# Subtracting the row maximum in a streaming softmax: one DVE maximum per tile, 12 tile buffers, unsplit last stores

## The chip, the cores and the metric

One core of a Trainium2 chip runs the kernel. The metric is device time in microseconds (us). TensorE is not used. In this document "tile t" is the t-th block of 512 rows (0 to 31), and DVE is VectorE, ACT is ScalarE, SP is SyncE.

## The reference

```python
x = np.random.randn(32, 512, 1024).astype(np.float32)   # temperature = 0.5

def reference(x, temperature):
    scaled = x / temperature
    shifted = scaled - np.max(scaled, axis=-1, keepdims=True)
    exp_x = np.exp(shifted)
    return (exp_x / np.sum(exp_x, axis=-1, keepdims=True)).astype(np.float32)
```

64 MiB come in and 64 MiB go out. A softmax does not depend on the shift, so the kernel before may leave the maximum out as long as no exponential overflows.

## The kernel before

A tile is 128 partitions of four rows of 1024 floats: 16 KiB per partition, 2 MiB in all. Everything is done in place in one of 8 buffers. Loads are issued from SP, stores from ACT, so there are two DMA queues. The tile framework orders the instructions of each engine at build time; each engine then takes its own list in that order and waits on semaphores (counters that other instructions raise) where data are not there yet.

```python
    data = ctx.enter_context(tc.tile_pool(name="data", bufs=8))
    ...
    for it, (g0, K) in enumerate(sched):            # 32 tiles, K = 4
        ...
        xtile = data.tile([P, K, d], mybir.dt.float32)
        nc.sync.dma_start(out=xtile.rearrange("p k d -> p (k d)"), in_=xv)   # line 47
        ...
        for j in range(K):
            nc.scalar.activation(                                            # line 52
                xtile[:, j, :], xtile[:, j, :],
                mybir.ActivationFunctionType.Exp,
                scale=scale, accum_out=sums[:, j : j + 1],
            )
        nc.vector.reciprocal(recip, sums)                                    # line 59
        for j in range(K):
            nc.vector.tensor_scalar_mul(                                     # line 61
                xtile[:, j, :], in0=xtile[:, j, :], scalar1=recip[:, j : j + 1]
            )
        if it >= ntiles - SPLIT_LAST and K > 1:     # last four tiles: store in two halves
            ...
        else:
            nc.scalar.dma_start(out=ov, in_=xtile)                           # line 70
```

The softmax here doesn't subtract the row's maximum and nothing guards it: scores larger than these inputs give would overflow.

Of the kernel before, what the change touches and what calls it, by code (L numbers as in the profile page):

```python
# [1 line left out]

# [4 lines left out]


@with_exitstack  # L10
def kernel(
    ctx: ExitStack,
    tc: tile.TileContext,
    x: bass.AP,
    temperature: bass.AP,
    out: bass.AP,
):
    nc = tc.nc
    scale = 1.0 / float(temperature)

    P = 128
    xf = x.flatten_outer_dims()
    of = out.flatten_outer_dims()
    n, d = xf.shape
    nrowgroups = n // P

    K_MAIN = 4
    SPLIT_LAST = 4
    sched = []
    g = 0  # L30
    while g < nrowgroups:
        k = min(K_MAIN, nrowgroups - g)
        sched.append((g, k))
        g += k
    ntiles = len(sched)

    data = ctx.enter_context(tc.tile_pool(name="data", bufs=8))
    stats = ctx.enter_context(tc.tile_pool(name="stats", bufs=16))

    for it, (g0, K) in enumerate(sched):  # L40
        rows = P * K
        r0 = g0 * P
        xv = xf[r0 : r0 + rows, :].rearrange("(p k) d -> p (k d)", p=P, k=K)
        ov = of[r0 : r0 + rows, :].rearrange("(p k) d -> p k d", p=P, k=K)

        xtile = data.tile([P, K, d], mybir.dt.float32)
        nc.sync.dma_start(out=xtile.rearrange("p k d -> p (k d)"), in_=xv)  # L47

        sums = stats.tile([P, K], mybir.dt.float32)
        recip = stats.tile([P, K], mybir.dt.float32)  # L50
        for j in range(K):
            nc.scalar.activation(  # L52
                xtile[:, j, :],
                xtile[:, j, :],
                mybir.ActivationFunctionType.Exp,
                scale=scale,
                accum_out=sums[:, j : j + 1],
            )
        nc.vector.reciprocal(recip, sums)  # L59
        for j in range(K):  # L60
            nc.vector.tensor_scalar_mul(  # L61
                xtile[:, j, :], in0=xtile[:, j, :], scalar1=recip[:, j : j + 1]
            )

        if it >= ntiles - SPLIT_LAST and K > 1:
            h = K // 2
            nc.scalar.dma_start(out=ov[:, :h, :], in_=xtile[:, :h, :])  # L67
            nc.sync.dma_start(out=ov[:, h:, :], in_=xtile[:, h:, :])
        else:
            nc.scalar.dma_start(out=ov, in_=xtile)  # L70


# [1 line left out]
_INS = ['x', 'temperature']  # L74
_OUTS = [((32, 512, 1024), 'float32')]
#: Inputs that are plain numbers.
_NUMBERS = {'temperature': 0.5}


# [26 lines left out]
```

## Time and profile before

| | before |
|---|---|
| time, median of 4 runs | 319.60 us (319.50 to 319.85) |
| span of the profiled run | 317.8 us |
| DMA, mean over the span | 422 GB/s |
| DVE busy / ACT busy | 93.4 / 138.0 us |

The span is the time from the first to the last instruction of the profiled execution.

These are lines of the page of the kernel before. Each row of digits has 40 slices of the span, a digit being the busy share in tenths (9 is 90% or more). The row GB/s is what DMA moved in each slice.

```profile
span 317.8 us, 636 instructions
...
DVE  0352333312300517631333213333123003733300
ACT  1875334554321739655334553345543106852500
...
DMA  7999999999999999999999999999999999999996
GB/s 297 429 394 429 431 431 434 435 433 433 433 429 429 432 429 429 429 429 431 429 433 434 433 435 431 429 433 431 431 429 429 431 429 431 437 429 430 422 426 271
...
DMA 91%; ACT 1%; SPq 1%; DVE 1%; issue 0%; DVEq 0%; ACTq 0%
```

The DMA row is full from the second slice to the last but one, and the chain that ended last (the last line) is 91% DMA. At about 431 GB/s a transfer of 2 MiB takes 4.87 us, and 64 of them take 312 us of the 317.8. DVE and ACT are idle more than half of the time, and that costs nothing.

The groups of instructions that matter (columns: line, engine, operation, output and input, count; then busy time and mean ns of one; then the idle time of the engine just before them):

```profile
L52 ACT ACTIVATE xtile<-xtile 128x1024 f32<-128x1024 f32 x128 | 133.5, 1044 | 159.3 <-DMA xtile<-in_x_dram 158.2
L61 DVE TENSOR_SCALAR xtile<-xtile,recip 128x1024 f32<-128x1024 f32 x128 | 87.7, 749 | 1.1
```

And the table of stretches: columns are the stretch and its length, busy time and count of DVE, ACT and POOL, clock, DMA share, GB/s.

```profile
100.00:160.00 60.00, 23.36 (x40) 34.62 (x65) 0.00 (x0) 1.00 1.01 431
160.00:280.00 120.00, 35.49 (x62) 51.95 (x98) 0.00 (x0) 1.00 1.01 431
280.00:290.00 10.00, 4.73 (x9) 4.26 (x8) 0.00 (x0) 1.00 1.01 430
290.00:300.00 10.00, 2.53 (x5) 4.27 (x8) 0.00 (x0) 1.00 1.00 424
```

DMA is as full at the end as in the middle. The last load has landed at 293.8 us (there ACT's last wait for a load ends); the stores still open then fill the remaining 24 us.

### The profile page before, as it was taken

Reading aid. Unit: us, or ns where it says so; the run is one execution under the profiler, and the core shown is the slowest. Engines: PE = TensorE matmul, PEld = TensorE weight load, DVE = VectorE, ACT = ScalarE, POOL = GpSimd, SP = SyncE. Lnnn points to the kernel's source line nnn. Section 1 sums busy time; section 2 is a strip of 40 time slices with the busy share of each in tenths; the row PEclk is TensorE's granted clock in tenths of the full one; section 3 lists DMA queues with packets and bytes.
Section 4 is the critical chain, followed back from the end, with each engine's and each line's share of the span. In section 5 each row is a group of like instructions: output and inputs, shape, how many; then the busy total and the mean of one; then the engine's idle time right before and its main releaser. Section 6 shows DMA issues by size and latency. Waiting matters only on the chain.

```text
span 317.8 us, 636 instructions
## 1 busy us (share of the span) xinstructions
DVE 93.4 (29%) x160; ACT 138.0 (43%) x257; POOL 0.2 (0%) x4
## 2 busy tenths in 40 slices
DVE  0352333312300517631333213333123003733300
ACT  1875334554321739655334553345543106852500
POOL 0000000000000000000000000000000000000000
DMA  7999999999999999999999999999999999999996
GB/s 297 429 394 429 431 431 434 435 433 433 433 429 429 432 429 429 429 429 431 429 433 434 433 435 431 429 433 431 431 429 429 431 429 431 437 429 430 422 426 271
DMA packets 9797, 134.26 MB, mean 422 GB/s; under 512 B 1088, under 2 KB 1088, under 8 KB 1088
## 3 DMA queue, kind: packets, MB, share of 16 engines
q1 hardware_dynamic: 5184, 71.31, 52.9%
q10 hardware_dynamic: 4608, 62.92, 46.3%
q14 instruction: 5, 0.04, 0.0%
HBM read 67.11 MB, written 67.11 MB: 422 GB/s over the span
## 4 chain that ended last, share of the span: by engine, by line
DMA 91%; ACT 1%; SPq 1%; DVE 1%; issue 0%; DVEq 0%; ACTq 0%
DMA xtile<-in_x_dram 55%; DMA out_dram<-xtile 36%; ACT xtile L52 1%; SPq L47 1%; DVE xtile L61 1%; DVEq L101 0%; ACTq L67 0%; DVE recip L59 0%; ACTq L52 0%; ACTq L70 0%
## 5 line engine op out<-in xcount | busy, mean ns | idle before, releaser
L52 ACT ACTIVATE xtile<-xtile 128x1024 f32<-128x1024 f32 x128 | 133.5, 1044 | 159.3 <-DMA xtile<-in_x_dram 158.2
L61 DVE TENSOR_SCALAR xtile<-xtile,recip 128x1024 f32<-128x1024 f32 x128 | 87.7, 749 | 1.1
L59 DVE RECIPROCAL recip<-sums 128x4 f32<-128x4 f32 x32 | 5.7, 178 | 206.5 <-ACT xtile L52 206.5
L52 ACT ACTIVATION_READ_ACCUMULATOR xtile<-xtile 128x1 f32 x128 | 23.8, 186 | 0.0
L52 ACT ACT_TABLE_LOAD x1 | 1.3, 1283 | 0.7 <-PEq L87 0.7
L87 POOL MEMSET const-bfloat16-1.0<- 128x1 bf16 x1 | 0.1, 101 | 0.0
L87 POOL MEMSET const-uint8-127<- 128x1 uint8 x1 | 0.1, 101 | 0.0
L87 POOL MEMSET const-float32-0.0<- 128x1 f32 x1 | 0.1, 98 | 0.2 <-issue 0.2
L87 POOL MEMSET const-float32-1.0<- 128x1 f32 x1 | 0.1, 98 | 0.0
## 6 DMA issues: line engine op xcount, KB each, us to landing
xtile<-in_x_dram SPq DMA_DIRECT2D x32, 2048.0 KB, 31.3
out_dram<-xtile ACTq DMA_DIRECT2D x28, 2048.0 KB, 24.2
out_dram<-xtile ACTq DMA_DIRECT2D x4, 1024.0 KB, 22.7
out_dram<-xtile SPq DMA_DIRECT2D x4, 1024.0 KB, 14.9
```

The source lines that it names most:

```text
L47: nc.sync.dma_start(out=xtile.rearrange("p k d -> p (k d)"), in_=xv)
L52: nc.scalar.activation(xtile[:, j, :], xtile[:, j, :], mybir.ActivationFunctionType.Exp, scale=scale, accum_out=sums[:, j : j + 1],)
L59: nc.vector.reciprocal(recip, sums)
L61: nc.vector.tensor_scalar_mul(xtile[:, j, :], in0=xtile[:, j, :], scalar1=recip[:, j : j + 1])
L87: nc = _bacc.Bacc("TRN2", target_bir_lowering=False, num_devices=1)
```

## The change

The intent is a softmax that cannot overflow: the row maximum is found on DVE and used as the bias of the exponential. The pool grows from 8 to 12 buffers, and the last stores are no longer split. The core of the diff:

```diff
+    nc.vector.tensor_reduce(                       # L17: maximum of four rows
+        out=top,
+        in_=xt[:, j0 : j0 + n, :],
+        axis=mybir.AxisListType.X,
+        op=mybir.AluOpType.max if scale > 0 else mybir.AluOpType.min,
+    )
+    nc.vector.tensor_scalar_mul(bias, in0=top, scalar1=-scale)     # L23
     for j in range(n):
-            nc.scalar.activation(... Exp, scale=scale, accum_out=...)
+        nc.scalar.activation(... Exp, bias=bias[:, j : j + 1], scale=scale, accum_out=...)   # L25
 ...
-    data = ctx.enter_context(tc.tile_pool(name="data", bufs=8))
+    data = ctx.enter_context(tc.tile_pool(name="data", bufs=12))
 ...
-        if it >= ntiles - SPLIT_LAST and K > 1:    (two half stores)
-        else:
-            nc.scalar.dma_start(out=ov, in_=xtile)
+            nc.scalar.dma_start(out=ov[:, j : j + k, :], in_=xt[:, j : j + k, :])            # L78
```

The diff does not show in which order DVE gets its instructions. That can be listed from the built program before anything runs. A piece of DVE's list, with the buffers' names replaced by tile numbers:

```
maximum 17, bias 17, maximum 18, bias 18, reciprocal 10, multiply 10 (x4)
maximum 19, maximum 20, reciprocal 11, bias 19, bias 20, multiply 11 (x4)
...
maximum 30, bias 30, maximum 31, reciprocal 21, bias 31, multiply 21 (x4)
```

We call "lead" how many tiles the latest maximum is ahead when tile t is multiplied. In the built program of the change it is, for t = 0, 1, 2, ...: 1, 2, 2, 3, 4, 4, 6, 6, 7, 7, 8, 9, 9, 10, 10, 9, 10, 9, 10, 10, 9, 10, and then falling by one per tile, as there are no more maxima.

More of the change, by code (lines that the diff above doesn't have):

```diff
@@ L7, with _softmax_rows @@
 from concourse._compat import with_exitstack
+def _softmax_rows(nc, stats, xt, j0, n, scale):
+    f32 = mybir.dt.float32
+    P = xt.shape[0]
+    top = stats.tile([P, n], f32, name="top")
+    bias = stats.tile([P, n], f32, name="bias")
+    sums = stats.tile([P, n], f32, name="sums")
+    recip = stats.tile([P, n], f32, name="recip")
+    nc.vector.tensor_reduce(
[5 more added lines that the diff above has]
+    nc.vector.tensor_scalar_mul(bias, in0=top, scalar1=-scale)
+    for j in range(n):
+        nc.scalar.activation(
+            xt[:, j0 + j, :],
+            xt[:, j0 + j, :],
+            mybir.ActivationFunctionType.Exp,
+            bias=bias[:, j : j + 1],
+            scale=scale,
+            accum_out=sums[:, j : j + 1],
+        )
+    nc.vector.reciprocal(recip, sums)
+    for j in range(n):
+        nc.vector.tensor_scalar_mul(
+            xt[:, j0 + j, :], in0=xt[:, j0 + j, :], scalar1=recip[:, j : j + 1]
+        )
 @with_exitstack
@@ L24 @@
     n, d = xf.shape
-    nrowgroups = n // P
-    K_MAIN = 4
-    SPLIT_LAST = 4
-    sched = []
-    g = 0
-    while g < nrowgroups:
-        k = min(K_MAIN, nrowgroups - g)
-        sched.append((g, k))
-        g += k
-    ntiles = len(sched)
-    data = ctx.enter_context(tc.tile_pool(name="data", bufs=8))
+    plan = [[4]] * 32
+    assert sum(sum(stores) for stores in plan) * P == n
+    data = ctx.enter_context(tc.tile_pool(name="data", bufs=12))
     stats = ctx.enter_context(tc.tile_pool(name="stats", bufs=16))
-    for it, (g0, K) in enumerate(sched):
+    r0 = 0
+    for stores in plan:
+        K = sum(stores)
         rows = P * K
-        r0 = g0 * P
-        xv = xf[r0 : r0 + rows, :].rearrange("(p k) d -> p (k d)", p=P, k=K)
+        xv = xf[r0 : r0 + rows, :].rearrange("(p k) d -> p k d", p=P, k=K)
         ov = of[r0 : r0 + rows, :].rearrange("(p k) d -> p k d", p=P, k=K)
-        xtile = data.tile([P, K, d], mybir.dt.float32)
-        nc.sync.dma_start(out=xtile.rearrange("p k d -> p (k d)"), in_=xv)
-        sums = stats.tile([P, K], mybir.dt.float32)
-        recip = stats.tile([P, K], mybir.dt.float32)
-        for j in range(K):
-            nc.scalar.activation(
-                xtile[:, j, :],
-                xtile[:, j, :],
-                mybir.ActivationFunctionType.Exp,
-                scale=scale,
-                accum_out=sums[:, j : j + 1],
-            )
-        nc.vector.reciprocal(recip, sums)
-        for j in range(K):
-            nc.vector.tensor_scalar_mul(
-                xtile[:, j, :], in0=xtile[:, j, :], scalar1=recip[:, j : j + 1]
-            )
-        if it >= ntiles - SPLIT_LAST and K > 1:
-            h = K // 2
-            nc.scalar.dma_start(out=ov[:, :h, :], in_=xtile[:, :h, :])
-            nc.sync.dma_start(out=ov[:, h:, :], in_=xtile[:, h:, :])
-        else:
-            nc.scalar.dma_start(out=ov, in_=xtile)
+        r0 += rows
+        xt = data.tile([P, K, d], mybir.dt.float32, name="xt")
+        nc.sync.dma_start(out=xt, in_=xv)
+        j = 0
+        for k in stores:
+            for a in range(j, j + k, 4):
+                _softmax_rows(nc, stats, xt, a, min(4, j + k - a), scale)
+            nc.scalar.dma_start(out=ov[:, j : j + k, :], in_=xt[:, j : j + k, :])
+            j += k
 _INS = ['x', 'temperature']
```

## The prediction

> **What bounds the kernel now.** DMA. The page's slices show the 16 DMA engines at 90% or more from the second slice to the last but one, at 429 to 435 GB/s; DVE is busy 29%, ACT 43%; the chain that ended last is 91% DMA. 64 transfers of 2 MiB at that rate are 4.87 us each, 312 us of the 317.8 us span. The bytes stay, so the change can only lose, by leaving DMA idle.
>
> **What is added.** Per tile one DVE maximum over 4096 elements. This trace has none; the Trainium skill ("VectorE: DVE Perf Modes", the perf-mode tier table) says tensor_reduce runs only at 1x, and gives the DVE clock as 0.96 GHz: estimate 4.3 us, 137 us in all. The trace's multiplies take 2.74 us for the same elements, which fits the table's 2x for fp32 tensor_scalar. DVE then has about 7.4 us per tile (maximum 4.3, bias and reciprocal 0.3, multiplies 2.74), some 235 us in all: under the 9.74 us per tile (load plus store) of DMA. By averages the change is hidden. ACT's bias adds perhaps 0.1 us per row, hidden too.
>
> **Where I expect the loss: program order on DVE.** In the built order the maxima run ahead of the multiplies, and the lead grows: multiply 0 stands behind maximum 1, multiply 7 behind 13, 11 behind 20, 13 behind 23, 16 behind 26, 18 behind 28, 21 behind 31. So from tile 11 on, store t waits until load t+9 or t+10 has landed, while load t+12 waits for store t to free one of 12 buffers. Only two or three tiles then circulate: maximum 4.3 + multiply 2.9, a store, a load, with about 2.5 us of issue and landing beyond each transfer's 4.87 us (before: load 0 issued by 1.1 us, ACT started at 8.5 us). Two tiles are 19.5 us of DMA work, one such round about 22 us.
>
> Walking the order by hand with these durations: DMA full until about 160 us, then gaps of 2 to 5 us every one or two tiles up to the last load, about 20 us in sum. The last load lands near 283 us. Then 11 stores (tiles 21 to 31) are still to come, and the first waits for maximum 31 and multiply 21: a gap of about 10 us. Then 11 x 4.87 = 54 us of pure stores, at DMA rate (ACT 4.5 us per tile), and 3 us of landing and end. Sum: span about 346, time about 347 us (the time is 1.8 us above the span before).
>
> The unsplit last stores cost nothing: stores are queued there. Twelve buffers give nothing, as eight already kept DMA full.
>
> **Prediction:** 347 us, 8 in 10 between 334 and 357. Faster by over 2%: 0.01; within 2%: 0.06; slower by over 2%: 0.93.
>
> **What would show it.** Maximum near 4.3 us; DVE about 235 us busy. DMA slices full in the first half, then 6 to 9 tenths up to about four fifths, one clear hole, then full to the end, stores only, at about 430 GB/s. The waits: DVE's maximum for loads, the SP queue's loads for stores, ACT's stores for the multiply. The last load lands over 55 us before the end (before: 24 us).
>
> **What would make it wrong.** If stores overlap loads better than in my walk (three tiles in circulation, not two), only the last hole remains: about 328 us. If the maximum is faster than 1x, the gaps shrink by up to half. If a lone transfer runs well below 430 GB/s, it is worse than 357.

## The result and the profile after

| | before | after |
|---|---|---|
| time, median of 4 runs | 319.60 us | 349.79 us (349.41 to 350.49) |
| ratio | | 1.0944 (95% interval 1.0929 to 1.0960) |
| span of the profiled run | 317.8 us | 347.6 us |
| DMA, mean over the span | 422 GB/s | 386 GB/s |
| DVE busy / ACT busy | 93.4 / 138.0 us | 234.5 / 149.1 us |

A ratio here is the mean time of one kernel's fast runs over that of the other's in the same rounds, so it is not quite the ratio of the medians in the table.

The same lines of the page after:

```profile
span 347.6 us, 655 instructions
...
DVE  0999949796589977498856855393594537666650
ACT  0665343207601517042092175019115701999930
...
DMA  8999999999999999999997799959858954999997
GB/s 300 428 415 426 430 441 424 424 436 435 424 434 434 430 424 439 428 428 413 388 381 300 332 332 432 422 213 393 381 241 307 439 219 184 445 428 422 422 421 334
...
DMA 69%; DVE 16%; ACT 9%; issue 3%; ACTq 0%; DVEq 0%; SPq 0%
```

DMA is full for the first half. Then the row has holes (the digits 7, 5, 8, 5, 4), and the GB/s row falls to 213 and 184 in single slices. After that it is full to the end. DVE is on the chain with 16% now, but it is not a full engine. Compare the rows: in slices 27 and 30 DMA has 5 and DVE 9, in slices 26 and 28 DVE has 3 and DMA 9. The two take turns, each waiting for the other.

The groups and stretches:

```profile
L25 ACT ACTIVATE xt<-xt,bias 128x1024 f32<-128x1024 f32 x128 | 145.3, 1136 | 176.1 <-DVE xt L35 124.6
L17 DVE TENSOR_REDUCE top<-xt 128x4 f32<-128x4096 f32 x32 | 141.2, 4415 | 83.2 <-DMA xt<-in_x_dram 83.2
L35 DVE TENSOR_SCALAR xt<-xt,recip 128x1024 f32<-128x1024 f32 x128 | 87.7, 748 | 0.5
```

```profile
100.00:160.00 60.00, 50.39 (x41) 19.67 (x34) 0.00 (x0) 1.00 1.01 431
160.00:280.00 120.00, 73.86 (x73) 48.29 (x84) 0.00 (x0) 1.00 0.88 354
280.00:290.00 10.00, 6.38 (x6) 0.00 (x0) 0.00 (x0) 1.00 0.26 109
290.00:300.00 10.00, 6.65 (x12) 5.81 (x11) 0.00 (x0) 1.00 0.87 367
300.00:340.00 40.00, 23.36 (x40) 33.65 (x58) 0.00 (x0) 1.00 1.00 426
```

This table is the whole loss. Against 431 GB/s, the 120 us at 354 GB/s hold (1 - 354/431) x 120 = 21.4 us of idle DMA, and the 20 us from 280 to 300 hold 7.5 + 1.5 = 9.0 us: together 30.4 us, and the spans differ by 29.8.

DVE sits idle for 83.2 us before maxima, waiting for loads. And loads (issued from SP at line 72) wait above all for stores, as this view of the SP queue's waits shows (who waited for whom, us in total, times, longest):

```profile
SPq L72 <- DMA out_dram<-xt: 185.3, 16, 22.5
SPq L72 <- DMA xt<-in_x_dram: 75.2, 10, 9.4
```

The second line, loads that wait for earlier loads, has another cause: the built program gives the 64 transfers eight semaphores by turns, and a transfer is issued only when the one that had its semaphore before has landed. Set against the landings in the trace, this ends the waits of loads 6 to 13, 15 and 16, the last at 89 us, while DMA is still full. From load 17 on, the wait that ends last is for the store that empties the load's buffer. So the eight semaphores do not make the loss.

A wait of loads for stores and of DVE for loads closes a ring only if stores wait for DVE. ACT, which issues the stores, does so for 124.6 us (the first group above ends its idle time with `DVE xt L35`, the multiply). The chain of waits shows the ring turning; columns are start, length, and what. In this chain and the later ones, pieces of 0.1 us and less are left out:

```profile
194.19 4.42 DVE top L17
198.60 2.65 DVE xt L35 x4
201.28 11.67 DMA out_dram<-xt
213.02 9.69 DMA xt<-in_x_dram
222.73 4.42 DVE top L17
227.27 2.74 DVE xt L35 x4
230.05 6.35 DMA out_dram<-xt
236.46 10.63 DMA xt<-in_x_dram
247.12 4.42 DVE top L17
```

One maximum (4.4 us), four multiplies (2.7 us), one store (11.7 us and then 6.4), one load (9.7 us and then 10.6, sharing the engines), and the next maximum may begin. Nothing in this ring is long. It hurts because so few tiles are in it at once.

### The profile page after: what moved, and what is told of

It is laid out like the page before. It is cut to its first block, busy times and chain, and to the rows that moved or that the text cites. A ratio compares the mean times of both kernels' runs of the same rounds, so it can differ in the third digit from the quotient of the medians.

```text
span 347.6 us, 655 instructions
## 1 busy us (share of the span) xinstructions
DVE 234.5 (67%) x224; ACT 149.1 (43%) x257; POOL 0.2 (0%) x4
## 2 busy tenths in 40 slices
DMA packets 9221, 134.26 MB, mean 386 GB/s; under 512 B 1024, under 2 KB 1024, under 8 KB 1024
## 4 chain that ended last, share of the span: by engine, by line
DMA 69%; DVE 16%; ACT 9%; issue 3%; ACTq 0%; DVEq 0%; SPq 0%
DMA xt<-in_x_dram 52%; DMA out_dram<-xt 17%; ACT xt L25 9%; DVE top L17 9%; DVE xt L35 7%; DVE recip L33 0%; ACTq L78 0%; DVEq L110 0%; DVE bias L23 0%; SPq L72 0%
## 5 line engine op out<-in xcount | busy, mean ns | idle before, releaser
L25 ACT ACTIVATE xt<-xt,bias 128x1024 f32<-128x1024 f32 x128 | 145.3, 1136 | 176.1 <-DVE xt L35 124.6
L17 DVE TENSOR_REDUCE top<-xt 128x4 f32<-128x4096 f32 x32 | 141.2, 4415 | 83.2 <-DMA xt<-in_x_dram 83.2
L35 DVE TENSOR_SCALAR xt<-xt,recip 128x1024 f32<-128x1024 f32 x128 | 87.7, 748 | 0.5
L25 ACT ACTIVATION_READ_ACCUMULATOR xt<-xt,bias 128x1 f32 x128 | 23.9, 186 | 0.0
L23 DVE TENSOR_SCALAR bias<-top 128x4 f32<-128x4 f32 x32 | 5.1, 165 | 0.4
```

The source lines that it names most:

```text
L17: nc.vector.tensor_reduce(out=top, in_=xt[:, j0 : j0 + n, :], axis=mybir.AxisListType.X, op=mybir.AluOpType.max if scale > 0 else mybir.Al ...
L23: nc.vector.tensor_scalar_mul(bias, in0=top, scalar1=-scale)
L25: nc.scalar.activation(xt[:, j0 + j, :], xt[:, j0 + j, :], mybir.ActivationFunctionType.Exp, bias=bias[:, j : j + 1], scale=scale, accum_o ...
L35: nc.vector.tensor_scalar_mul(xt[:, j0 + j, :], in0=xt[:, j0 + j, :], scalar1=recip[:, j : j + 1])
```

## The experiments

The theory: a buffer is released by its store, a store needs its multiply, and in DVE's list the multiply of tile t stands behind the maximum of tile t + lead. So the load of tile t + lead must land before store t can begin, while the load of tile t + buffers waits for store t. What circulates are buffers - lead tiles; we call that the slack. With slack 2 the DMA engines are given too little to do. The rivals: the maximum's own 4.4 us per tile, the unsplit last stores, the larger pool.

All experiments start from the changed kernel. Order on DVE is imposed with edges that order issue and add no wait:

```diff
+def _behind(tc, later, earlier):
+    tc.add_manual_dep(later, earlier.name,
+        mybir.DependencyInfo(mybir.DependencyClass.NoSync, mybir.DependencyReason.DATA),
+        reason="order on DVE")
```

Here `maxima[t]` is the maximum of tile t and `multiplies[t]` its four multiplies. All kernels gave the right result.

The edges hold DVE's list alone. ACT's list is built anew and is not the same in all runs: in e6, for one, the exponentials run five tiles ahead of the stores, in e5, once its start is over, one tile. That does not make the difference: no instruction of ACT stands on the change's chain of waits between 89 and 293 us, nor on e6's between 100 and 380 us.

| run | buffers | lead | slack | median us | ratio to before |
|---|---|---|---|---|---|
| e8_lead11 | 12 | 11 | 1 | 556.13 | 1.740 |
| e6_b8_lead6 | 8 | 6 | 2 | 414.42 | 1.298 |
| e7_lead10 | 12 | 10 | 2 | 400.22 | 1.253 |
| e4_b8 | 8 | grows to 5 and 6 | 2 to 3 | 375.25 | 1.174 |
| the change | 12 | grows to 9 and 10 | 2 to 3 | 349.79 | 1.094 |
| e3_split | 12 | as the change | 2 to 3 | 350.64 | 1.097 |
| e9_lead9 | 12 | 9 | 3 | 336.67 | 1.053 |
| e2_order_cheap | 12 | as the change | 2 to 3 | 332.68 | 1.040 |
| e10_lead8 | 12 | 8 | 4 | 322.69 | 1.010 |
| e5_lead6 | 12 | 6 | 6 | 319.24 | 0.999 |
| e1_lead1 | 12 | at most 1 | 11 | 322.08 | 1.007 |
| e11_b8_cap3 | 8 | at most 3 | 5 | 319.56 | 1.000 |

Lead and slack are for the tiles before the end, where the maxima run out.

### e1_lead1: all the work, another order

```diff
+    for t in range(len(maxima) - 1 - 1):
+        _behind(tc, maxima[t + 1 + 1], multiplies[t][-1])
```

> The changed kernel with every operation kept (12 buffers, full maximum, unsplit stores); only the order of issue on DVE is held so that maxima are never more than one tile ahead of the multiplies. Theory (the growing lead of the maxima starves DMA): no gaps, 320 us (318 to 323), DVE still about 234 us busy. Rival 1 (the maximum's work or its latency per tile is the cost): stays near 350 us.

Measured: 322.08 us, ratio 1.0071 (1.0056 to 1.0086), with DVE 235.5 us busy. The same work on the same engines, with the order on DVE held, gives back 27.7 of the 30.2 us. Rival 1 falls. The last 2.4 us are real: in the stretch from 300 to 310 us the DMA engines moved only 270 GB/s. There DVE goes from tile to tile without idle time (7.39 us each) right up to the last load's maximum, which begins at 300.8 us, so little is queued for storing when loads run out. It is late because it stood still before, for 27.9 us up to 172 us, as two lines of the view of waits show:

```profile
ACT xt L25 <- DMA xt<-in_x_dram: 54.1, 4, 32.8
DVE recip L33 <- ACT xt L25: 45.1, 3, 27.9
```

Here the eight semaphores do bind: by the built program store 13 has the semaphore that load 20 had before, load 20 landed at 170.0 us, and only at 170.1 us did ACT issue store 13 and go on to its next exponentials. Whether e1 would be at full speed without this was not tested.

### e2_order_cheap: the order alone, nearly without the work

```diff
-        in_=xt[:, j0 : j0 + n, :],
+        in_=xt[:, j0 : j0 + n, :64],
+    LEAD = [1, 2, 2, 3, 4, 4, 6, 6, 7, 7, 8, 9, 9, 10, 10, 9, 10, 9, 10, 10, 9, 10, 9, 8, ...]
+    for t, lead in enumerate(LEAD):
+        for m in multiplies[t]:
+            _behind(tc, m, maxima[t + lead])
+        if t + lead + 1 < len(maxima):
+            _behind(tc, maxima[t + lead + 1], multiplies[t][-1])
```

The maximum of 64 columns is a valid shift too, so the result stays right.

> The changed kernel's order on DVE forced tile by tile, but the maximum reads only 64 of 1024 columns (about 0.45 us instead of 4.4; the result stays right, as any shift cancels). Theory (order times length of the round): two tiles' round shrinks to about 18 us, under the 19.5 us that DMA needs, so the gaps in the middle nearly vanish, and the hole after the last load shrinks from 10 to about 6 us: 326 us (322 to 334). If order alone were the cause, whatever the length: 350. If only the work were: 320.

Measured: 332.68 us. With the maximum cut from 4415 to 420 ns and DVE only 33% busy, the order alone still costs 13 us, 43% of the change's loss. So neither the order alone nor the work alone is the cost: it is the order, times the length of the ring. The size was misjudged (326 expected, inside the range of 322 to 334): gaps in the middle did not nearly vanish. From its table of 10 us stretches, 160 to 270 us hold about 8.8 us of idle DMA and 270 to 280 us another 4.5. On e2's chain the rounds from maximum to maximum take 26.4 us (191.78 to 218.16) and 21.1 us (to 239.22) where about 18 was expected. Their loads take 14.7 and 10.2 us and their stores 8.1 and 7.3, with other transfers under way beside them; lone ones take 7.6 and 6.3 (e8 below). The expectation had reckoned with lone transfers.

### e3_split: the last stores split again

> The changed kernel with the last four stores split over two queues, as before the change. Theory: stores are queued at the end, nothing gained: 350 us (348 to 352). Rival 2 (the unsplit last stores cost the time): falls towards 320.

The edit is the branch of the kernel before, for the last four tiles. Measured: 350.64 us. Rival 2 falls: the stores are queued at the end, and halves of them arrive no sooner.

### e4_b8: 8 buffers, order left to the scheduler

```diff
-    data = ctx.enter_context(tc.tile_pool(name="data", bufs=12))
+    data = ctx.enter_context(tc.tile_pool(name="data", bufs=8))
```

> The changed kernel with 8 buffers instead of 12, order left to the scheduler; the built order again has the maxima two buffers short of the pool (lead 5 and 6 of 8), and reaches that from tile 6 on instead of tile 13. Theory: gaps start at about 110 us instead of 160, so slower still: 356 us (345 to 365). Rival 3 (the 12 buffers themselves hurt): falls towards 320. Rival 4 (buffers help, more would be better, order irrelevant): also slower, so this run tells only rival 3.

Measured: 375.25 us, slower than the range said. Rival 3 falls: under this order the 12 buffers do not hurt, they are worth 25 us. The built lead follows the pool: it stops at two short of it (10 of 12, 6 of 8), so the smaller pool reaches slack 2 sooner. Page lines of this run:

```profile
span 373.5 us, 666 instructions
...
DMA  8999999999869978958995899598699769919997
```

The holes begin in slice 11, at about 93 us (10 slices of 9.3 us), instead of slice 22 of the change's row, at about 182 us (21 slices of 8.7 us).

### e5_lead6 and e6_b8_lead6: the same lead, two pools

```diff
+    for t in range(len(maxima)):
+        for m in multiplies[t]:
+            _behind(tc, m, maxima[min(t + 6, len(maxima) - 1)])
+    for t in range(len(maxima) - 6 - 1):
+        _behind(tc, maxima[t + 6 + 1], multiplies[t][-1])
```

e6 has `bufs=8` besides.

> 12 buffers, every operation as in the changed kernel; the maxima held exactly 6 tiles ahead of the multiplies from the first tile on. Slack theory (what counts is buffers less lead, here 6 tiles in circulation): no gaps in the middle and stores queued at the end, 320 us (318 to 324). Rival (the length of the lead alone delays the stores): like the next run with the same lead, far above 350.

> 8 buffers, maxima held exactly 6 tiles ahead: slack 2. Slack theory: two tiles circulate from the first store on. Walked by hand: the two fall in step (one store alone, then a store and a load sharing the engines), 27 us per two tiles, last load near 370, then a hole and seven stores: 417 us (385 to 430). Rival (lead alone): same as the run with 12 buffers and lead 6.

Measured: 319.24 us with 12 buffers (ratio 0.9985, interval 0.9968 to 1.0002) and 414.42 us with 8. The lead is the same, 6 tiles from the first tile on; only the slack differs, 6 against 2. Here is what e5 shows on its page:

```profile
span 317.6 us, 672 instructions
...
DVE  0899999996779777788777797677977769756640
...
DMA  8999999999999999999999999999999999999996
```

DVE does all the work of the change (236 us of it), and the DMA row is as full as before the change. What counts is not how far ahead the maxima run, but how many buffers are left beyond that.

### e7_lead10 and e8_lead11: slack 2 from the start, and slack 1

The edit is that of e5, with 10 or 11 in place of 6.

> 12 buffers, maxima held exactly 10 tiles ahead: slack 2 from the first store on, where the changed kernel gets there only from tile 13. Slack theory: same 27 us per two tiles, last load near 335, then a hole and eleven stores: 402 us (375 to 415).

> 12 buffers, maxima held exactly 11 tiles ahead: slack 1, so load, maximum, multiply, store of one tile after another. Slack theory: a round of 7.5 (DVE) + 7.4 (store) + 7.4 (load) = 22.3 us per tile, last load near 508, then twelve stores: 580 us (560 to 600). Rival (DVE work is the cost, order is not): near 350.

Measured: 400.22 and 556.13 us. In e7 every second maximum in the trace begins at 146.90, 173.92 and 200.67 us: 27.0 and 26.8 us per two tiles, as walked by hand, against the 19.5 us that DMA needs for them. The chain of waits of e7 shows why it is not the 21 us of an undisturbed round:

```profile
173.92 4.42 DVE top L17
178.34 2.65 DVE xt L36 x4
181.02 10.72 DMA out_dram<-xt
191.79 8.86 DMA xt<-in_x_dram
200.67 4.42 DVE top L17
```

The store takes 10.7 us and the load 8.9 in this ring, against 6.3 and 7.6 when nothing else is on the engines. Those lone values are read from e8's chain, where one tile is in the ring at a time:

```profile
104.82 4.42 DVE top L17
109.24 2.65 DVE xt L36 x4
111.92 6.28 DMA out_dram<-xt
118.25 7.58 DMA xt<-in_x_dram
125.86 4.42 DVE top L17
```

This round is 21.0 us where 22.3 was expected: the store took 6.3 us instead of 7.4 and DVE 7.1 instead of 7.5, and the load 7.6 instead of 7.4. Over about 20 rounds 1.3 us are 26 us, which accounts for the 580 us expected and the 556 measured (just below the range). DVE is busy 42% of the time in e8 and no engine is anywhere near full: pure latency.

### e9_lead9 and e10_lead8: slack 3 and 4

The edit is that of e5, with 9 or 8.

> 12 buffers, maxima held exactly 9 tiles ahead: slack 3. A round without contention was about 21 us with slack 1; three tiles in it carry 29 us of DMA work, so the middle is nearly full, and only a part of the hole after the last load is left, as stores 20 and 21 are at work then. Slack theory: 328 us (320 to 336).

> 12 buffers, maxima held exactly 8 tiles ahead: slack 4. Slack theory: 320 us (318 to 325).

Measured: 336.67 us (its four runs spread from 335.1 to 339.3, and its median is just above the range) and 322.69 us. By 21.0 us of an undisturbed round, three tiles should keep DMA full, as they carry 29.2 us of work. They do not quite: in its table of 10 us stretches, those from 60 to 100 us hold 342, 356, 405 and 367 GB/s, and later ones go down to 360. Its chain has maxima at 121.20, 152.58 and 183.55 us, so a round with three tiles on the way takes 31 us, not 21: its stores take 8.4 and 14.2 us and its loads 10.1 and 15.4. By estimate, 29.2 us of work in 31 are 406 GB/s, and the table's stretches from 100 to 270 us have 409 on average. Why three tiles together take that long was not tested. Slack 4 has only the hole after the last load: 238 GB/s from 270 to 280 us, worth 4.5 us.

### e11_b8_cap3: the maximum, with the old pool

```diff
-    data = ctx.enter_context(tc.tile_pool(name="data", bufs=12))
+    data = ctx.enter_context(tc.tile_pool(name="data", bufs=8))
+    for t in range(len(maxima) - 3 - 1):
+        _behind(tc, maxima[t + 3 + 1], multiplies[t][-1])
```

> 8 buffers as before the change, every other operation of the changed kernel, maxima at most 3 tiles ahead: slack 5 or more. Slack theory: full speed again with the old number of buffers, 320.5 us (318.5 to 323), where the scheduler's own order with 8 buffers took 375.

Measured: 319.56 us, ratio 0.9998 (0.9983 to 1.0013). The same pool took 375.25 us in e4 with the scheduler's own order. The safe softmax is free, with 8 buffers, once its maxima are kept from running too far ahead. With this rival 4 of e4 falls too: order is not irrelevant.

No version that beats the kernel before clearly came up: e5, at 0.9985, is the nearest, and its interval includes 1. Of the 317.8 us, 312 are transfer.

## Why the prediction was right

- **What bounds.** Right: DMA before the change, and after it DMA starved by a ring of waits rather than a busier engine. DVE is 67% busy after, and e5 and e11 run at full speed with 74 and 75%.
- **The maximum.** 4.3 us estimated, 4.415 measured. This agrees with the Trainium skill, "VectorE: DVE Perf Modes", the perf-mode tier table, which has tensor_reduce at 1x only: by estimate, 4096 elements at that page's 0.96 GHz are 4.27 us, and 0.15 us are left over. The multiply took 748 ns for 1024 elements, which fits the table's 2x for fp32 tensor_scalar (by the same estimate 533 ns at 2x, 1067 at 1x).
- **The bias on ACT.** "Perhaps 0.1 us per row": 1044 became 1136 ns, 92 ns more. The Trainium skill, "ScalarE: Activation LUTs", section "What ACT_TABLE_LOAD costs", gives about 93 ns for each such operand. It was hidden.
- **Where the time went.** About 20 us of gaps before the last load and a hole of about 10 us after it were forecast; 21.4 and 9.0 us were measured. The last maximum begins at 283.6 us ("near 283"). That the gaps came out so near looks in part like luck. The prediction put a round at about 22 us; on the change's chain above, the rounds from maximum to maximum take 28.5 and 24.4 us. Of the prediction's terms (7.2 us on DVE, 7.4 per transfer), the one on DVE was right (7.1 and 7.3), while the transfers took 6.4 to 11.7 us, with others beside them. The record does not say how far the walk by hand let transfers overlap.
- **Why.** e1, e5 and e11 show that the order on DVE makes the loss, with all operations kept. e5 against e6 shows that it acts through the slack. e2 shows that the maximum's length counts only inside that ring: it takes the loss from 13 to 30 us.
- **The unsplit stores** cost nothing (e3), as said.

What was off:

- "About 2.5 us of issue and landing beyond each transfer's 4.87 us" was read from the first load. For a lone load it holds (7.58 - 4.87 = 2.7), for a lone store it is 1.4 us.
- "Twelve buffers give nothing" was right only for an order that leaves slack. Under the built order they are worth 25 us (e4).
- "If the maximum is faster than 1x, the gaps shrink by up to half": a nearly free maximum leaves 13 of 30 us, so a little more than half goes away.
- The sum was 2.8 us short (347 against 349.8), which no single term explains.

What stays open is why the scheduler lets the lead grow until two buffers are left. The built programs show that it does, with 8 and with 12 buffers; no run shows the reason.

## What to carry to other kernels

When a change puts a second operation per tile on an engine that executes in order, look at the built order of that engine, not only at its busy share: if the early operation may run ahead of the late one, every tile of lead takes a buffer out of circulation. Count buffers less lead, multiply out the ring (early operation, late operation, store, load, each with its issue and landing), and ask whether that many tiles per round give the bound engine enough to do. If not, try an order edge before more buffers: with 8 buffers it cost nothing here and was worth 56 us (e11 against e4), where four more buffers were worth 25.

## What the Trainium skill lacked or had wrong

- "Perfetto Trace Analysis", section "Optimization Strategy", takes consistent bubbles as a sign that there may not be enough SBUF for the next tile. More buffers did help here (25 us for four, e4), but the order was at fault: with it mended 8 buffers ran in 319.6 us where 12 had taken 349.8. The section says nothing of the order in which an engine's instructions are built.
- "Perfetto Trace Analysis", section "Identifying the Most-Contended Engine", judges DVE and ACT by occupancy. After the change DVE has the higher of the two, 67%, but the same work at 74 and 75% (e5, e11) costs no time. The section judges DMA by throughput, and by that DMA stays the most contended in both kernels. Neither points to the cause here.
- "DMA: Bandwidth & Descriptors", section "Anatomy of one DMA — SWDGE (gpsimd) path", fits one fixed cost of about 2.0 us to transfers issued from GpSimd; the section has no fit for those issued from SP and ACT. From release to release, a lone store of 2 MiB issued from ACT took 6.28 us and a lone load issued from SP 7.58 us (e8); with 4.87 us of transfer that leaves 1.4 and 2.7 us. Their mean is near the 2.0, but stores and loads differ.
- The same page, section "Where 436 GB/s comes from", says that HBM at about 358 GB/s, a core's half of a stack's 716, binds transfers between HBM and SBUF, next to a measured 425. That does not hold for one core at work: this kernel, loading and storing at once, held 429 to 435 GB/s.
